# A two-layer encoder step: two more feed-forward tile buffers, the last gate's place, the tail weights' split and the norms' engines

## The chip, the cores and the metric

The kernel runs on one core of a Trainium2 chip, as one launch. The metric is the device time of that launch in microseconds (us). Engines: TensorE (PE; PEld is its weight load), VectorE (DVE), ScalarE (ACT), GpSimd (POOL) and SyncE (SP), which issues most of the DMAs. Each engine works through its instructions in the order in which the program emits them.

## The reference

A prompt of 1024 frames and a sample of 32 frames (T = 1056 columns here) go through two layers of width 1024. The first layer's mixer is a matrix-memory recurrence, the second one's is a sliding-window attention. After each mixer, and after each feed-forward block, comes a post-normalisation. The part that the change touches is this:

```python
def layer_norm(x, g, b):
    mu = jnp.mean(xf, -1, keepdims=True)
    var = jnp.mean(jnp.square(xf - mu), -1, keepdims=True)
    return (xf - mu) * lax.rsqrt(var + LN_EPS) * g + b

def swiglu(x, w_gu, w_down):            # D_FF = 2816
    g, u = jnp.split(x @ w_gu, 2, axis=-1)
    return (jax.nn.silu(g) * u) @ w_down

for layer in range(DEPTH):              # DEPTH = 2
    mix = mixer(layer, x)               # mLSTM, then sliding-window attention
    x = layer_norm(DEEPNORM_ALPHA * x + mix, ln_g[layer, 0], ln_b[layer, 0])
    x = layer_norm(DEEPNORM_ALPHA * x + swiglu(x, w_gu[layer], w_down[layer]),
                   ln_g[layer, 1], ln_b[layer, 1])
```

## The kernel before, in words

Everything is kept transposed: features on the 128 partitions, frames along the free axis. `ACT` holds the residual stream, `SX` its split into a rounded high part and a low part (fp32r). A product of two f32 matrices is three fp32r matmuls: high times high, high times low, low times high (L361, L362, L363 in `gemm`).

**Weights.** `Weights` streams them: SP loads a raw tile `wr` (three buffers), ScalarE casts the high part `wh` (L201), and GpSimd or, for the keys in `on_vector`, VectorE subtracts to get the low part `wl` (L203). Five such pairs of slots exist, and some weights have a home elsewhere (`ex`). For pairs of units, VectorE also makes sums of weights (L174 to L180). A raw tile is loaded anew when its last subtraction has read it. `done` releases a factor and emits the next ones at once.

**Order.** The program is emitted by Python generators. `Weave.tick` is called from `gemm` with an estimate of the time of three matmuls and steps each launched task when its pause has run out; `drain` runs a task at once to its end or to a condition. So what a task yields decides where its instructions stand in each engine's queue, not when they run.

**Feed-forward.** The 1056 columns are four quarters of 264 (`N4`). Tiles 0 and 1 of the 22 are made plainly, tiles 2 to 21 by `up_tile` with seven products in place of eight (a Strassen-like scheme) into PSUM banks A and B. Each tile takes buffers of `Z` from the list `free`: `s0` for the gate, `su0`, `su1` for the up parts, `s1` for the second gate. `alloc` takes one, and when none is free it drains the oldest staging task until one is. `stage(p)` combines tiles 2p and 2p+1, splits each combination (L1269 cast, L1270 subtraction) into buffers 7 to 10 in turn, and sends it to DRAM (`hs`, L1271); a buffer of the two tiles comes free with t1, x11, t4 and x22. The last Silu of a tile and its product (L1370, L1371) are in the task `rest`, which is launched after the last product. `behind` is set for the last tile alone: it starts loading the staged tiles back (L1413) while that tile is made.

The down product runs over four blocks with seven products each (`down`, L1465 and L1467 add into `ACT`), and a fifth, the tail, is done plainly for one quarter after the other (`run` in `ffn`, L1525), with the eight tail units `dn[TAIL]` from `dnt`.

**Norms.** `norm_tail` makes the quarters and launches `ln_task` for each. Its `li` is 1 and 3 behind the feed-forward blocks of the two layers. Per quarter: partial sums (L601, L603), a matmul with `onesm` for the mean (L422), centring (L427), squares (L429), their sums (L431, L434), a matmul for the variance (L438), the reciprocal root (L444 to L449), scaling (L453, L459 to L463), and the split for the next product (L469, L475). `LN_PACE` gives the pauses, `LN_LAG` adds to the one ahead of the variance matmul. In the last norm of the kernel quarter 2 is made with the pauses of `RUSH` (`rush`), and quarter 3 by `LastNorm`. After layer 0 the key, value and query products of the attention run between the steps of the last norms (`keys_values`, `q_group`); the attention's first steps come behind them (L1693 scores, L1699 their sums with the bias).

Of the kernel before, what the change touches and what calls it, by code (L numbers as in the profile page):

```python
# [9 lines left out]
F32 = mybir.dt.float32  # L10
# [6 lines left out]
P = 128  # L17
# [37 lines left out]
    ((4.2, 0.9, 1.1, 4.4, 1.0, 1.4, 0.8), (4.2, 0.7, 0.9, 4.2, 0.8, 1.4, 0.8)),  # L55
)

LN_LAG = {(2, 0): 7.0}

RUSH = (3.2, 0.8, 0.6, 2.8, 0.8, 1.0, 0.6)  # L60

# [3 lines left out]
N4 = T // 4  # L65
# [176 lines left out]
def kernel(ctx: ExitStack, tc: tile.TileContext, A, O):  # L242
# [14 lines left out]
    def new(p, tag, shape, dt=F32, bufs=1):  # L257
        uid[0] += 1
        return p.tile(list(shape), dt, name=f"{tag}_{uid[0]}", tag=tag, bufs=bufs)
# [29 lines left out]
    def add_ffn(layer):  # L289
        up, dn = {}, []  # L290
        for c, i in VISITS:
            held = up.get((i, 1 - c)) if i == FIRST - 1 else None
            up[i, c] = held or [add("gu", 2 * (layer * FT + i) + k) for k in range(2)]
        for i in range(FIRST, FT):
            up[i] = add_pair("gu", 2 * (layer * FT + i))
        for b in range(TAIL):
            dn.append([add_pair("dn", 4 * (layer * TAIL + b) + 2 * j) for j in range(2)])
        dn.append([add("dnt", KT * layer + m) for m in range(KT)])
        on_vector.update((u, 1) for u in dn[TAIL])
        on_vector.update((u, f) for i in range(FIRST) for c in range(2) for u in up[i, c] for f in range(2))  # L300
        U_UP.append(up)
        U_DN.append(dn)
# [100 lines left out]
    def ln_task(z_, lps, grp, li, last, final):  # L403
        cols, (c, zs) = grp
        w = cols.stop - cols.start

        rush = final and grp is QUARTERS[2]
        y = RUSH if rush else LN_PACE[li & 1][last]
        acc = z_[:, 0:2, c, zs]
        sq = [acc] + [z_[:, 2 + 2 * i : 4 + 2 * i, c, zs] for i in range(3)]  # L410
        rs, r2 = z_[:, 8, c, zs], z_[:, 9, c, zs]
        n = KT // 2

        def z2(kk):
            return ACT[:, 2 * kk : 2 * kk + 2, cols]

        def s2(i, kk):
            return SX[:, i, 2 * kk : 2 * kk + 2, cols]

        yield y[0]  # L420
        pm = new(lps, "ln", [P, 512], bufs=3 if li & 1 else 2)[:, :w]
        nc.tensor.matmul(pm, onesm[:], acc[:, 0, :], start=True, stop=True)  # L422
        yield y[1]
        for s in range(n + 2):
            if s < n:

                nc.vector.tensor_sub(z2(s), pm.unsqueeze(1).broadcast_to([P, 2, w]), z2(s))  # L427
            if 1 <= s <= n:
                nc.scalar.activation(sq[s - 1], z2(s - 1), AF.Square)  # L429
            if s >= 3:  # L430
                (nc.gpsimd if rush or li & 1 and not (last or s & 1) else nc.vector).tensor_add(acc, acc, sq[s - 2])  # L431
            yield y[2]
        if not rush:
            nc.vector.tensor_add(acc[:, 0], acc[:, 0], acc[:, 1])  # L434
        yield y[3] + LN_LAG.get((li, cols.start // N4), 0.0)
        pv = new(lps, "ln", [P, 512], bufs=3 if li & 1 else 2)[:, :w]
        for i in range(1 + rush):
            nc.tensor.matmul(pv, onesm[:], acc[:, i, :], start=(i == 0), stop=(i == rush))  # L438
        squared.add((li, cols.start // N4))
        yield y[4]  # L440

        if not li & 1:
            nc.scalar.preload_act_table_set("natural_log_exp_and_others")
        nc.scalar.activation(rs, pv, AF.Ln, bias=eps_ln[:])  # L444
        nc.scalar.activation(rs, rs, AF.Exp, scale=-0.5)
        nc.scalar.activation(r2, rs, AF.Square, scale=0.5 ** 0.5)
        yield y[5]
        nc.vector.scalar_tensor_tensor(r2, pv, eps_ln[:], r2, op0=ALU.add, op1=ALU.mult)
        nc.vector.scalar_tensor_tensor(rs, r2, 1.5, rs, op0=ALU.subtract, op1=ALU.mult)  # L449
        for s in range(n + 3):  # L450
            if s < n:
                eng = nc.gpsimd if rush and s & 1 else nc.vector
                eng.tensor_mul(z2(s), z2(s), rs.unsqueeze(1).broadcast_to([P, 2, w]))  # L453
            kk = s - 1
            if 0 <= kk < n:
                for k in (2 * kk, 2 * kk + 1):
                    z, gk, bk = ACT[:, k, cols], lng[:, li, k : k + 1], lnb[:, li, k : k + 1]
                    if rush and k & 1:
                        nc.gpsimd.tensor_scalar(z, z, gk, bk, op0=ALU.mult, op1=ALU.add)  # L459
                    elif li & 1 and last and k & 1:  # L460
                        nc.vector.tensor_scalar(z, z, gk, bk, op0=ALU.mult, op1=ALU.add)
                    else:
                        nc.scalar.activation(z, z, AF.Identity, scale=gk, bias=bk)  # L463
            kk = s - 2
            if 0 <= kk < n:
                if final:
                    nc.sync.dma_start(O["y"][:, 2 * kk : 2 * kk + 2, cols], z2(kk))
                else:
                    nc.scalar.copy(s2(0, kk), z2(kk))  # L469
                    if li == 1:  # L470
                        nc.scalar.dma_start(scr[:, 2 * kk : 2 * kk + 2, cols], z2(kk))
            kk = s - 3
            if kk >= 0 and not final:
                eng = nc.gpsimd if kk & li & 1 else nc.vector
                eng.tensor_sub(s2(1, kk), z2(kk), s2(0, kk).bitcast(F32))  # L475
            yield y[6]

    class LastNorm:
# [574 lines left out]
    class Mixer(ExitStack):  # L1053
# [3 lines left out]
        def __init__(self, closing, us):  # L1057
            super().__init__()
            closing()
            psx[0].close()  # L1060
            dense_psum(4)
            self.ex, self.zx = ExitStack(), ExitStack()
            self.E = new(self.ex.enter_context(pool("ex")), "ex", [P, 2, 3 * KT // 2, HALF], F32R)
            self.z = new(self.zx.enter_context(pool("z", side="right")), "z", [P, 11, 2, N4])
            self.lnps = self.enter_context(pool("lnps", PSUM, side="right"))
            self.made, self.plain, self.left = [], [False, False], 0
            for i, u in zip((0, 4, 1, 5, 2, 3), us):
                for f in range(2):
                    W.home[u, f] = [self.E[:, h, 2 * i + f, : D // 2] for h in range(2)]
# [149 lines left out]
    def ffn(layer, li, tasks, lx, final):  # L1219
# [19 lines left out]
        def tiles(t):  # L1239
            return [(t[:, 0, k, :], t[:, 1, k, :]) for k in range(t.shape[2])]  # L1240

        free = list(range(6))
        kept = {}
        staging = []
        turn = [0]
# [8 lines left out]
        def buf(i):  # L1256
            return Z[:, i, :, :]
# [65 lines left out]
        def up_tile(i, behind=None):  # L1323
            u = up[i]

            def mul(ps, f, o, **kw):
                w = tiles_of(W.factor(u, f))
                if i == FIRST and o[0] == "t":
                    summed(o)
                for c in range(2):  # L1330
                    gemm(ps[:, c, :], w, tiles(X[o](c)), **kw)
                W.done(u, f)
                if behind:
                    behind(o)

            a = bank("A")
            mul(a, "a1", "x11")
            finish_tile()
            s0 = alloc()
            gate0 = buf(s0)  # L1340
            nc.scalar.copy(gate0, a)
            if i > FIRST and not i % 2:
                staging.append(wv.launch(stage(i // 2 - 1)))
            b = bank("B")
            mul(b, "a2", "x21")
            nc.vector.tensor_add(gate0, gate0, b)
            nc.scalar.activation(gate0, gate0, AF.Silu)
            mul(a, "s2", "t2", again=True)
            su0 = alloc()
            up0 = buf(su0)  # L1350
            nc.scalar.copy(up0, a)
            b = bank("B")
            mul(b, "b2", "t4")
            nc.vector.tensor_add(up0, up0, b)
            mul(a, "s1", "t1", again=True)
            su1 = alloc()
            up1 = buf(su1)
            nc.scalar.copy(up1, a)  # L1358
            b = bank("B")
            mul(b, "s3", "t3")  # L1360
            nc.vector.tensor_add(up0, up0, b)
            nc.vector.tensor_add(up1, up1, b)
            nc.vector.tensor_mul(gate0, gate0, up0)
            free.append(su0)
            mul(a, "s4", "x22", again=True)
            s1 = alloc()
            kept[i] = s0, s1

            def rest():
                nc.scalar.activation(buf(s1), a, AF.Silu)  # L1370
                nc.vector.tensor_mul(buf(s1), buf(s1), up1)  # L1371
                free.append(su1)
                yield 0.5

            tail.append(wv.launch(rest()))
# [595 lines left out]
```

## Time and profile before

| | us |
|---|---|
| runs, median of 3 | 2244.7 |
| lowest and highest | 2244.04, 2245.94 |
| profiled execution, its own time | 2244.99 |
| its span, first to last instruction | 2242.9 |
| TensorE busy in it | 2187.7 |
| VectorE busy | 1472.7 |
| ScalarE busy | 999.6 |
| GpSimd busy | 1018.3 |

The profile is of one execution. A row of the waits gives who waited for whom, the time in all, how often, and the longest. A row of a timeline gives the start in us from the span's beginning, the duration, engine, line, operation and tiles, and in brackets how long the engine was idle before and what ended that. A row of the windows gives the stretch, its length, and for PE, PEld, DVE, ACT and POOL the busy time and the instructions in it, then the granted clock of TensorE, the busy share of the DMA engines, and GB/s. A row of the groups gives the count, the busy time, the mean in ns, and idle time before them. L203 is line 203 of the kernel before.

### The profile page before, as it was taken

The page shows a single profiled execution, that of the slowest core. Times are in us where ns is not written, and L with a number is a line of the kernel's source. Part 1 is how long each engine was busy: PE and PEld are TensorE (multiplying, and loading weights), DVE is VectorE, ACT ScalarE, POOL GpSimd, SP SyncE. Part 2 cuts the span into 40 slices and gives each one's busy share as a digit, 9 for nine tenths or more (in the row PEclk, how much of TensorE's full clock was granted, in tenths as well). Part 3 has the DMA queues.
Part 4 walks back from the last instruction along what each step waited for, and adds up shares of the span by engine and source line. Part 5 has one row for each costly group of instructions (what it writes and reads, how often), then busy time and mean ns, then how long its engine had stood idle before and what let it go on. Part 6 is the DMA issues. An engine that isn't in the chain of part 4 may idle for free.

```text
span 2242.9 us, 44249 instructions
## 1 busy us (share of the span) xinstructions
PE 2187.7 (98%) x17086; PEld 2151.6 (96%) x17086; DVE 1472.7 (66%) x2864; ACT 999.6 (45%) x2253; POOL 1018.3 (45%) x961
## 2 busy tenths in 40 slices
PE   9999999999999999999998999899999999999997
PEld 9899999999999999999998999899999999999997
DVE  4465576777566665566667678888666666456657
ACT  4443355465344444322246678656444444332124
POOL 2544331003665666545326676400566666554422
PEclk9999999999999999999999999999999999999999
DMA  4222112211443443697425433421344434397712
GB/s 149 75 54 69 53 40 86 96 39 58 165 138 140 154 152 137 230 332 232 153 79 169 115 99 95 138 78 39 106 154 160 139 134 154 135 347 242 257 50 78
DMA packets 174499, 298.10 MB, mean 133 GB/s; under 512 B 18065, under 2 KB 130761, under 8 KB 174289
## 3 DMA queue, kind: packets, MB, share of 16 engines
q1 hardware_dynamic: 169936, 290.94, 39.1%
q10 hardware_dynamic: 4352, 4.33, 0.6%
q8 instruction: 135, 2.21, 0.4%
q14 instruction: 76, 0.61, 0.1%
HBM read 201.80 MB, written 82.94 MB: 127 GB/s over the span
## 4 chain that ended last, share of the span: by engine, by line
PE 80%; DVE 8%; ACT 4%; DMA 3%; issue 3%; POOL 1%; SPq 0%; ACTq 0%; DVEq 0%; POOLq 0%
PE A L361 9%; PE A L363 9%; PE A L362 9%; PE d L361 8%; PE d L363 8%; PE d L362 8%; PE B L361 7%; PE B L362 7%; PE B L363 7%; PE T L1737 1%; DMA wr<-in_dn 1%; ACT act L463 1%; PE T L906 1%; PE O L1752 1%; DVE wl L203 1%
## 5 line engine op out<-in xcount | busy, mean ns | idle before, releaser
L203 POOL TENSOR_TENSOR wl_s<-wr,wh_s 128x512 fp32r<-128x512 f32 x224 | 316.6, 1434 | 243.0 <-ACT wh_s L201 182.6
L361 PE MATMUL d<-sx,wh 128*128 128x264 f32 (+2 forms) x1068 | 341.1, 319 | 0.7 <-DVE act L1525 0.7
L363 PE MATMUL d<-sx,wl 128*128 128x264 f32 (+2 forms) x1068 | 326.2, 305 | 1.4 <-POOL wl L203 1.4
L362 PE MATMUL d<-sx,wh 128*128 128x264 f32 (+2 forms) x1068 | 325.3, 305 | 0.1
L203 POOL TENSOR_TENSOR wl_a<-wr,wh_a 128x512 fp32r<-128x512 f32 x112 | 169.0, 1515 | 331.2 <-ACT wh_a L201 329.5
L201 ACT CAST wh_s<-wr 128x512 fp32r<-128x512 f32 x224 | 135.4, 617 | 310.9 <-DVE wr L178 279.4
L361 PE MATMUL A<-sx,wh_s 128*128 128x264 f32 x896 | 255.4, 285 | 3.5 <-ACT z L1358 3.5
L362 PE MATMUL A<-sx,wh_s 128*128 128x264 f32 x896 | 254.9, 284 | 0.0
L363 PE MATMUL A<-sx,wl_s 128*128 128x264 f32 x896 | 254.8, 284 | 0.0
L361 PEld LDWEIGHTS d<-sx,wh 128*128 128x128 f32 x1068 | 202.6, 190 | 4.3 <-ACT z L444 1.1
L363 PEld LDWEIGHTS d<-sx,wl 128*128 128x128 f32 x1068 | 201.6, 189 | 2.5 <-POOL wl L203 2.2
L362 PEld LDWEIGHTS d<-sx,wh 128*128 128x128 f32 x1068 | 202.3, 189 | 1.1 <-DVE sx L392 0.4
L363 PE MATMUL d<-sx,ex 128*128 128x264 f32 x624 | 177.7, 285 | 3.5 <-DVE ex L203 3.5
L361 PE MATMUL d<-sx,ex 128*128 128x264 f32 x624 | 180.6, 289 | 0.4 <-ACT sx L391 0.2
L203 POOL TENSOR_TENSOR wl<-wr,wh 128x512 fp32r<-128x512 f32 (+2 forms) x75 | 100.1, 1344 | 177.5 <-ACT wh L201 154.5
L362 PE MATMUL d<-sx,ex 128*128 128x264 f32 x624 | 177.3, 284 | 0.3 <-DVE sx L392 0.2
L361 PEld LDWEIGHTS A<-sx,wh_s 128*128 128x128 f32 x896 | 169.3, 189 | 4.0 <-ACT z L1358 4.0
L363 PEld LDWEIGHTS A<-sx,wl_s 128*128 128x128 f32 x896 | 169.6, 189 | 0.0
L362 PEld LDWEIGHTS A<-sx,wh_s 128*128 128x128 f32 x896 | 169.2, 189 | 0.0
L1270 POOL TENSOR_TENSOR z<-z 128x528 fp32r<-128x528 f32 x76 | 105.3, 1385 | 109.2 <-issue 58.0
L1717 POOL TENSOR_SCALAR s<-s,st 128x256 f32<-128x256 f32 (+1 forms) x144 | 126.6, 891 | 61.3 <-DVE st L1715 47.6
L1269 ACT CAST z<-z 128x528 fp32r<-128x528 f32 x136 | 85.9, 631 | 95.5 <-DVE z L1282 44.9
(338 smaller groups left out, 7299.3 us busy)
## 6 DMA issues: line engine op xcount, KB each, us to landing
wr<-in_gu SPq DMA_DIRECT2D x92, 512.0 KB, 4.9
hs_x<-z SPq DMA_DIRECT2D x72, 528.0 KB, 2.8
hs_t<-z SPq DMA_DIRECT2D x64, 528.0 KB, 2.9
sx<-hs_x SPq DMA_DIRECT2D x112, 264.0 KB, 5.9
sx<-hs_t SPq DMA_DIRECT2D x64, 264.0 KB, 6.4
ex<-hs_t SPq DMA_DIRECT2D x64, 264.0 KB, 6.4
wr<-in_dn SPq DMA_DIRECT2D x32, 512.0 KB, 3.9
ex<-hs_x SPq DMA_DIRECT2D x32, 264.0 KB, 5.9
```

Of the source, the lines that this page charges most:

```text
L201: self.nc.scalar.copy(hi, r)
L203: eng.tensor_sub(lo, r, hi.bitcast(F32))
L361: nc.tensor.matmul(out, ah, bh, start=start and k == 0, stop=False, **kw)
L362: nc.tensor.matmul(out, ah, bl, start=False, stop=False, **kw)
L363: nc.tensor.matmul(out, al, bh, start=False, stop=stop and k == last, **kw)
L463: nc.scalar.activation(z, z, AF.Identity, scale=gk, bias=bk)
L906: nc.tensor.matmul(pc[:, : 2 * (DV + 1)], keys, vt[j][:L, c], start=True, stop=True)
L1269: nc.scalar.copy(hi.bitcast(F32R), buf(s))
L1270: eng.tensor_sub(lo.bitcast(F32R), buf(s), hi)
L1717: nc.gpsimd.tensor_scalar_mul(p[:R, h, lo:256], p[:R, h, lo:256], st[:R, 2, h : h + 1])
L1737: nc.tensor.transpose(pt[:nk, i, h, :R], p[:R, h, c : c + nk], ident[:R, :R])
L1752: nc.tensor.matmul(po[:, :, :R], v, s["hi"][:nk, i, :, :R], start=(i == 0), stop=False)
```

## The change

The buffer `Z` has 13 tiles in place of 11, and the list `free` starts with eight buffers in place of six. In the last tile the second gate's Silu is emitted behind its last product and ahead of `W.done`, which emits the next weights' casts; in the other tiles it stays in `rest`. The second half of the tail weights is no longer in `on_vector`, so GpSimd makes both low parts. In `ln_task` the additions L431 stay on GpSimd in the rushed quarter alone; of the scalings, L453 and the odd steps of the rushed quarter leave GpSimd (for VectorE and ScalarE), and all of L475 is on VectorE. `LN_LAG` adds 1.0 and 1.2 us of ticks ahead of the variance matmul in quarters 2 and 3 behind the first feed-forward block.

```diff
-LN_LAG = {(2, 0): 7.0}
+LN_LAG = {(1, 2): 1.0, (1, 3): 1.2, (2, 0): 7.0}
...
         dn.append([add("dnt", KT * layer + m) for m in range(KT)])
-        on_vector.update((u, 1) for u in dn[TAIL])
...
             if s >= 3:
-                (nc.gpsimd if rush or li & 1 and not (last or s & 1) else nc.vector).tensor_add(acc, acc, sq[s - 2])
+                (nc.gpsimd if rush else nc.vector).tensor_add(acc, acc, sq[s - 2])
...
             if s < n:
-                eng = nc.gpsimd if rush and s & 1 else nc.vector
-                eng.tensor_mul(z2(s), z2(s), rs.unsqueeze(1).broadcast_to([P, 2, w]))
+                nc.vector.tensor_mul(z2(s), z2(s), rs.unsqueeze(1).broadcast_to([P, 2, w]))
...
-                    if rush and k & 1:
-                        nc.gpsimd.tensor_scalar(z, z, gk, bk, op0=ALU.mult, op1=ALU.add)
-                    elif li & 1 and last and k & 1:
+                    if li & 1 and last and k & 1:
                         nc.vector.tensor_scalar(z, z, gk, bk, op0=ALU.mult, op1=ALU.add)
...
             if kk >= 0 and not final:
-                eng = nc.gpsimd if kk & li & 1 else nc.vector
-                eng.tensor_sub(s2(1, kk), z2(kk), s2(0, kk).bitcast(F32))
+                nc.vector.tensor_sub(s2(1, kk), z2(kk), s2(0, kk).bitcast(F32))
...
-            self.z = new(self.zx.enter_context(pool("z", side="right")), "z", [P, 11, 2, N4])
+            self.z = new(self.zx.enter_context(pool("z", side="right")), "z", [P, 13, 2, N4])
...
-        free = list(range(6))
+        free = [*range(6), 11, 12]
...
-            def mul(ps, f, o, **kw):
+            def mul(ps, f, o, then=None, **kw):
...
                 for c in range(2):
                     gemm(ps[:, c, :], w, tiles(X[o](c)), **kw)
+                if then:
+                    then()
                 W.done(u, f)
...
-            mul(a, "s4", "x22", again=True)
             s1 = alloc()
             kept[i] = s0, s1
 
+            def gate1():
+                nc.scalar.activation(buf(s1), a, AF.Silu)
+
+            mul(a, "s4", "x22", behind and gate1, again=True)
+
             def rest():
-                nc.scalar.activation(buf(s1), a, AF.Silu)
+                if not behind:
+                    gate1()
                 nc.vector.tensor_mul(buf(s1), buf(s1), up1)
                 free.append(su1)
                 yield 0.5
```

## The prediction

> **What bounds the kernel now.** I read the busy shares of the page first, then the waits of TensorE, then the windows around each long wait, then the timelines there.
>
> ```profile
> PE 2187.7 (98%) x17086; PEld 2151.6 (96%) x17086; DVE 1472.7 (66%) x2864; ACT 999.6 (45%) x2253; POOL 1018.3 (45%) x961
> ```
>
> The waits of TensorE (in all, times, longest, us), those that the change can touch:
>
> ```profile
> PE psS L1693 <- DVE st L1699: 3.7, 2, 3.1
> PE A L361 <- ACT z L1358: 3.5, 2, 1.9
> PE d L363 <- DVE ex L203: 3.5, 6, 1.1
> PE A L361 <- ACT z L1370: 3.0, 2, 1.8
> ...
> PE ln L438 <- DVE z L434: 2.1, 2, 1.1
> PE ln L555 <- DVE z L544: 2.1, 1, 2.1
> ```
>
> TensorE (PE) is the bound: busy 98%. Its matmuls do not change, so only its waits are to be had; 2242.9 − 2187.7 = 55 us is idle, start and end included. Six kinds of wait are shown, and each edit aims at one or two. Next to them stands what a quiet stretch looks like:
>
> ```profile
> 560.00:580.00 20.00, 18.07 (x136) 17.86 (x135) 10.00 (x12) 7.54 (x15) 11.62 (x10) 0.91 0.54 188
> 600.00:620.00 20.00, 20.00 (x167) 20.00 (x166) 12.23 (x14) 8.36 (x16) 12.59 (x9) 1.00 0.44 162
> 940.00:960.00 20.00, 18.78 (x155) 18.57 (x154) 12.80 (x17) 6.07 (x11) 11.68 (x8) 1.00 1.08 374
> 1180.00:1200.00 20.00, 18.30 (x105) 17.66 (x105) 15.87 (x27) 10.81 (x21) 9.02 (x9) 0.91 0.42 131
> 1600.00:1620.00 20.00, 18.38 (x152) 18.17 (x151) 9.94 (x13) 8.39 (x16) 11.97 (x9) 1.00 0.54 189
> 1980.00:2000.00 20.00, 18.17 (x150) 17.96 (x149) 12.86 (x18) 6.33 (x12) 11.68 (x8) 1.00 1.06 354
> ```
>
> A full 20 us holds 167 matmuls of this shape, 0.12 us each. Missing matmuls times 0.12 is therefore the true loss of a stretch, with pipeline drain and lowered clock in it.
>
> **Two more buffers (free list of 8).** Tiles 0 and 1 keep four of the six buffers; every later tile takes four (`s0`, `su0`, `su1`, `s1`) and returns two. From the code this is arithmetic on ticks: a product is 8 ticks of 0.339 = 2.7, a tile seven products = 19.0; the staging of a pair returns a buffer at ticks 2, 12.4, 28 and 33.2 (t1, x11, t4, x22). An odd tile asks for `su1` after five of its products, 19.0 + 13.6 = 32.6 after the even tile began, and what it gets is the buffer of t4. Pairs from 1 on start staging one product into an even tile: 2.7 + 28 = 30.7, in time. Pair 0 starts after four products of tile 2: 10.8 + 28 = 38.8, too late. So once per layer, in tile 3, `alloc` finds the list empty and drains two puts back to back. With eight buffers one is left even there, and no drain occurs.
>
> ```profile
> 570.10 0.63 ACT L1269 CAST z<-z 128x528 fp32r<-128x528 f32 x1 [4.58 <-DMA hs_t<-z]
> 571.56 0.60 ACT L1358 COPY z<-A 128x528 f32<-128x528 f32 x1 [0.83 <-DVE z L1270]
> ```
>
> The drained put sits ahead of the copy that frees bank A: ScalarE waits 4.58 us for the earlier put's DMA, then for VectorE, and TensorE waits 1.9 us for the copy. Gone with the drain are (167 − 136) × 0.12 = 3.7 us in layer 0 (half of it the clock: 0.91 over 20 us is 0.09 × 20 = 1.8) and (167 − 152) × 0.12 = 1.8 in layer 1: **−5.5**. Next late: the put of x22 now falls 5.4 ticks behind that of t4, on the same staging buffer, and one round trip there was 4.58 us of waiting plus work; a late landing would hold ScalarE some 2 us, but the copy behind it has one whole product (24 × 0.12 = 2.9 us) before its bank is used. So nothing is charged; if that cover failed, 2 us a layer.
>
> The Trainium skill (TensorE: Matmul & The Clock Gate, section on HAM oscillation) would have the clock fall only for idle gaps above some 3.4 us. This trace differs: 0.91 follows a 1.9 us wait. By the page the sum below would be 1.8 us smaller; the measured row decides.
>
> **Last gate ahead of the release.** The last tile's Silu (L1370) frees bank A for the first down product, but is emitted behind a weight cast.
>
> ```profile
> 945.91 0.62 ACT L201 CAST wh_s<-wr 128x512 fp32r<-128x512 f32 x1 [3.45 <-PE A L363]
> 946.44 0.60 ACT L1370 ACTIVATE z<-A 128x528 f32<-128x528 f32 x1
> ```
>
> The same stretch on VectorE and GpSimd, then the chain some 10 us later:
>
> ```profile
> 945.13 0.69 DVE L178 TENSOR_TENSOR wr<-wr,wr 128x512 f32<-128x512 f32 x1
> 947.08 1.38 DVE L1371 TENSOR_TENSOR z<-z 128x528 f32<-128x528 f32 x1 [1.25 <-ACT z L1370]
> 947.85 1.80 POOL L1270 TENSOR_TENSOR z<-z 128x528 fp32r<-128x528 f32 x1
> ```
>
> ```profile
> 957.86 6.82 DMA wr<-in_dn
> 964.68 0.28 issue
> 964.96 0.69 DVE wr L174
> 965.65 0.63 DVE act L1465
> ```
>
> The cast waits for L178, which ends at 945.82, while ScalarE idles 3.45 us in which the Silu fits; behind it now stands that cast, which L178 holds until then anyway. Losses removed: (167 − 155) × 0.12 = 1.4 and (167 − 150) × 0.12 = 2.0. But I read on for what is late next. At 957.86 SP, in its order behind the last pair's staging puts, issues the next down weights (6.82 us); then comes L174, and behind it on VectorE the L1465 that frees bank A again. Coming 1.4 or 2.0 us earlier, it waits for the same load. That chain starts from L1270; L1371 runs beside it until 948.46, 0.6 of its 1.80 us, and will now run before it. So only about 0.5 us a layer stays: **−1.0**, bounds 0 and −3.4; I take the low part as the DMA share is 1.08 there.
>
> **Tail weights on GpSimd alone.** Of the 8 tail units a layer, the second half's subtraction leaves VectorE.
>
> ```profile
> L203 POOL TENSOR_TENSOR ex<-wr,ex 128x384 fp32r<-128x384 f32 x6 | 6.1, 1018 | 13.9 <-ACT ex L201 13.9
> ```
>
> ```profile
> 1116.09 0.43 DVE L1525 TENSOR_TENSOR act<-act,d 128x264 f32<-128x264 f32 x1 [1.76 <-PE d L363]
> 1116.44 1.35 DVE L203 TENSOR_TENSOR ex<-wr,ex 128x384 fp32r<-128x384 f32 x1
> ```
>
> VectorE is not slow, it is in the wrong order: L203 for a unit to come stands behind L1525, which waits for TensorE's end of the unit before (1.76). Raw loads wait for these subtractions too. GpSimd has 13.9 us idle before its six, so six more of 1.02 (6.1) fit; a pair takes 2.04 against a unit's 18 × 0.12 = 2.2 us. With raw buffers freed by GpSimd, it runs units ahead; behind its subtractions stand only those of the next weights. The waits were 3.5 us on matmuls in two layers; resuming costs about 0.1 each time, six times: **−4.2**. Bounds −3.5 and, GpSimd late, the rival below.
>
> **Norms on VectorE, two held steps.**
>
> ```profile
> L475 DVE TENSOR_TENSOR sx<-act,sx 128x528 fp32r<-128x528 f32 x40 | 30.0, 760 | 14.0 <-ACT sx L469 14.0
> ...
> L431 POOL TENSOR_TENSOR z<-z 128x528 f32<-128x528 f32 x8 | 10.6, 1326 | 63.9 <-ACT z L429 63.0 <-DVE z L431 0.7
> ```
>
> And on VectorE, at quarters 2 and 3 of the first layer:
>
> ```profile
> 1184.27 0.71 DVE L431 TENSOR_TENSOR z<-z 128x528 f32<-128x528 f32 x1 [1.19 <-POOL z L431]
> ...
> 1217.64 1.80 DVE L475 TENSOR_TENSOR sx<-act,sx 128x528 fp32r<-128x528 f32 x1
> ```
>
> Five of the eight L431 and all eight L475 of GpSimd (steps 1 and 3 of four quarters) move, 0.75 each on VectorE. In layer 0 that is 3 + 8 = 11 × 0.75 = 8.3 us more work. Against it, VectorE waited 1.19 for one L431, and lost 1.80 − 0.76 = 1.0 when its L475 ran beside GpSimd's. At quarter 2 it gains 1.19 and what is shortened, less two operations of 0.7: about 0.4. The held matmul (1.0 tick, two steps of the next product; L444 to L449 of its norm stand behind it) no longer stands in the way, but the bank of that product waits for VectorE as well. At quarter 3 the hold of 1.2 removes the 1.1 us wait for L434, yet TensorE then comes earlier to the attention's scores, where it waits 3.1 for L1699, the end of the same norm chain; I credit 0.6 for a chain not interrupted. Together **−1.0**. Bounds: +3 (both holds delay the chain, 2.2, and 0.8 of backlog) and −2.7 (the second half-speed stretch, 0.91 at 1180, is not entered: 1.7 more). I take the middle, since every wait here ends on VectorE.
>
> The rushed norm of the last layer moves two L453 to VectorE and four scale steps to ScalarE, just ahead of TensorE's last long wait.
>
> ```profile
> L453 DVE TENSOR_TENSOR act<-act,z 128x528 f32<-128x528 f32 x2 | 1.4, 704 | 0.0
> ```
>
> ```profile
> 2223.68 1.31 DVE L540 TENSOR_TENSOR z<-z,act 128x528 f32<-128x528 f32 x1
> ...
> 2227.32 1.41 DVE L544 TENSOR_TENSOR z<-z 128x264 f32<-128x264 f32 x1
> 2228.65 0.42 DVE L558 TENSOR_TENSOR act<-act,d 128x264 f32<-128x264 f32 x1
> ```
>
> VectorE gets 1.4 us more (2 × 704 ns), and L540 (0.6) and L544 (1.0) shrink to free durations (0.7, and 0.42 as L558 has it), with 0.3 between: 1.9 back, **−0.5**. Bounds: 0, if ScalarE with its four steps comes late with the squares in between, and −0.8.
>
> **Sum.** −5.5 − 1.0 − 4.2 − 1.0 − 0.5 = −12.2. The profiled execution took 2244.99 (its span 2242.9), the median of the runs is 2244.7: 2244.99 − 12.2 = 2232.8, rounded to 2233.0.
>
> **The rivals.**
> 1. *More is kept.* The down weights also land earlier (2.4 us more of the gate's 3.4) and the half-speed stretch at 1187 goes (1.7): 2228.9. Against it: DMA share 1.08.
> 2. *GpSimd becomes the bound of the tail.* Its L1270 above took 1.80, 0.6 of it beside VectorE's work; 1.02 in that measure (× 1.5, half of it hidden: × 1.37) is 1.4, which makes a pair 2.8 against 2.2. Six units lose 3.6 a layer, less one unit's lead (2.2): 4.2 + 2 × 1.4 = 7.0 given back, 2240.0. It decides once a subtraction exceeds 1.1. The Trainium skill (SBUF — State Buffer, section Who interferes with whom) has this as a rule: two-operand VectorE work and GpSimd's reads exclude each other, and the one issued first wins. For it speaks L203's 1.35 us on VectorE; against, the six rows' mean of 1018.
> 3. *The buffers do not do what they say*, a drain still being forced somewhere: 5.5 back, 2238.5. Against it: the count has one drain, and the view has one wait per layer.
> 4. *Slower: VectorE's backlog in the first layer's norms reaches the attention.* All 11 moved operations (8.3) and both holds (2.2) land on the chain that ends in L1699, its longer waits lower the clock three more times (3 × 1.7), and the 1.0 is lost: 16.6 back, 2249.6. It decides once the backlog passes 12 us. For it: VectorE busy 15.87 of 20 us at 1180. Against: 4.13 us were idle there, and GpSimd's share blocked it anyway.
>
> **How the numbers follow.** Chances: forecast 0.62, rival 1 0.14, rival 2 0.09, rival 3 0.06, rival 4 0.05, other small losses between 2237 and 2243 0.04. The range 2226.5 to 2239.5 takes in the forecast with the bounds of its norms and gate terms, rivals 1 and 3. About 0.2% (4.5 us) is what a measurement of this kernel can tell from no change: faster needs less than 2240.5. That is forecast, rivals 1 and 3 and most of rival 2: 0.88. Same gets 0.08; slower, past 2249.5, 0.04.
>
> **What would show it.** Right: no wait of TensorE for L1358's counterpart, and granted clock 1.00 around 570; none on `ex` from L203; no wait for the last Silu, but a longer one, 1.5 to 2 us, for L1465 some 20 us later in both layers; the wait for L1699 grown towards 4 us while those for L434 are gone; L544 near 0.5. Wrong: waits of TensorE on GpSimd's `ex`, new clock losses between 1180 and 1440, or a wait in tile 3 or 4 of either layer.

## The result: 6 us faster, half of the forecast, and the profile after

| | before | after |
|---|---|---|
| median of 12 runs each, us | 2244.43 | 2238.71 |
| lowest to highest | 2240.66 to 2246.44 | 2236.94 to 2240.69 |
| ratio, 95% interval | | 0.9973 (0.9966 to 0.9981) |
| profiled execution, its span | 2244.99, 2242.9 | 2237.53, 2235.7 |

The ratio is 6.1 us (4.3 to 7.6) off 2244.7. Forecast were 12, to 2233.0, with a range of 2226.5 to 2239.5: the sign held and the time is inside the range, near its slow end. Later ratios are likewise turned into us by 2244.7, since the kernel before drifted from 2244 to 2247 between the groups of runs.

In the changed kernel the lines have moved: `gemm` is L360 to L362, the squares' sums L430 and L433, the split L470, the tail's eviction L1527, the copies L1338, L1348 and L1355, the down additions L1467 and L1469, the scores' sums L1701. TensorE's waits in the profile after (in all, times, longest, us):

```profile
PE psS L1695 <- DVE st L1701: 5.7, 1, 5.7
...
PE A L360 <- DVE act L1467: 3.3, 2, 1.7
...
PE d L360 <- DVE act L1527: 2.3, 1, 2.3
PE d L362 <- POOL wl L203: 2.1, 3, 0.8
...
PE ln L550 <- DVE z L539: 1.3, 1, 1.3
PE ln L437 <- DVE z L433: 1.3, 1, 1.3
...
PE A L360 <- ACT z L1348: 1.1, 2, 0.7
```

Gone are the waits on `ex`, for the last Silu and for L1358's counterpart (L1355). In their place stand a longer one for the down additions, a new one (L1348), the one for the tail's eviction (L1527), grown from 0.7 to 2.3, and one of 5.7 for the scores' sums. Two of the prediction's own signs of being wrong are there: L1348 is a wait in tile 4 of both layers, and the clock at 1200 to 1220 is 0.90 where it was 1.00 (at 1180 to 1200 it is 1.00 where it was 0.91). By windows (columns as before):

```profile
560.00:580.00 20.00, 20.00 (x167) 20.00 (x166) 9.68 (x12) 7.75 (x14) 11.18 (x9) 1.00 0.39 134
580.00:600.00 20.00, 19.28 (x159) 19.07 (x158) 11.79 (x15) 9.35 (x17) 12.72 (x11) 1.00 0.56 190
940.00:960.00 20.00, 20.00 (x167) 20.00 (x167) 13.82 (x21) 6.21 (x12) 12.41 (x9) 1.00 1.08 374
960.00:980.00 20.00, 18.38 (x152) 18.20 (x151) 13.21 (x21) 4.25 (x7) 9.36 (x7) 1.00 1.07 378
1200.00:1220.00 20.00, 12.81 (x71) 12.29 (x72) 17.64 (x26) 11.64 (x26) 13.28 (x11) 0.90 0.76 223
```

TensorE runs the same 17086 matmuls in both traces, almost in the same order, so one can ask where the same matmul starts in each. Its shift (after minus before), read on the level stretches ahead of each place and behind it, gives the account; a third number is what is left of a gain some 15 to 20 us later:

| stretch | shift from, to (us) | the change's term | forecast |
|---|---|---|---|
| ahead of the first feed-forward | 0, +0.97 | +1.0 | 0 |
| buffers, layer 0 (572; then 588) | +0.97, −2.77, −1.77 | −2.7 | −3.7 |
| gate, layer 0 (947; then 966) | −1.77, −3.25, −1.82 | −0.1 | −0.5 |
| tail weights, layer 0 | −1.80, −4.55 | −2.75 | −2.1 |
| norms and attention (1135 to 1235; by 1600) | −4.55, −2.38, −2.23 | +2.3 | −1.0 |
| buffers, layer 1 (1613; then 1628) | −2.23, −4.08, −3.33 | −1.1 | −1.8 |
| gate, layer 1 (1987; then 2006) | −3.33, −5.43, −3.84 | −0.5 | −0.5 |
| tail weights, layer 1 | −3.83, −6.33 | −2.5 | −2.1 |
| end | −6.33, −7.13 | −0.8 | −0.5 |

The first row is code that the change doesn't touch, so it is put down to chance between two executions. Without it this pair of traces gives −8.1; the timed runs say −6.1. Such chance is in the other rows too, above all between 1135 and 1600, where the clock falls two to four times in every trace.

### The profile page after: what moved, and what is told of

It is laid out like the page before. It is cut to its first block, busy times and chain, and to the rows that moved or that the text cites. A ratio compares the mean times of both kernels' runs of the same rounds, so it can differ in the third digit from the quotient of the medians.

```text
span 2235.7 us, 44254 instructions
## 1 busy us (share of the span) xinstructions
PE 2182.9 (98%) x17086; PEld 2149.4 (96%) x17086; DVE 1468.5 (66%) x2863; ACT 999.8 (45%) x2257; POOL 1008.0 (45%) x958
## 4 chain that ended last, share of the span: by engine, by line
PE 62%; DVE 4%; issue 2%; DMA 2%; ACT 2%; POOL 1%; SPq 0%; ACTq 0%; POOLq 0%; DVEq 0%
PE A L360 9%; PE A L362 9%; PE A L361 9%; PE B L360 6%; PE B L361 6%; PE B L362 6%; PE d L360 4%; PE d L362 4%; PE d L361 4%; PE T L1739 1%; DMA wr<-in_dn 1%; PE psS L1695 1%; PE O L1754 1%; PE psS L1696 1%; PE O L1755 1%
## 5 line engine op out<-in xcount | busy, mean ns | idle before, releaser
L360 PE MATMUL d<-sx,wh 128*128 128x264 f32 (+2 forms) x1068 | 341.4, 320 | 3.3 <-DVE act L1527 2.3
L362 PE MATMUL d<-sx,wl 128*128 128x264 f32 (+2 forms) x1068 | 326.0, 305 | 2.2 <-POOL wl L203 2.1
L360 PE MATMUL A<-sx,wh_s 128*128 128x264 f32 x896 | 254.9, 284 | 1.1 <-ACT z L1348 1.1
L362 PE MATMUL A<-sx,wl_s 128*128 128x264 f32 x896 | 254.0, 284 | 0.0
L360 PEld LDWEIGHTS d<-sx,wh 128*128 128x128 f32 x1068 | 202.3, 189 | 7.0 <-issue 2.8
L203 POOL TENSOR_TENSOR wl<-wr,wh 128x512 fp32r<-128x512 f32 (+2 forms) x79 | 104.7, 1333 | 224.3 <-ACT wh L201 210.2
L362 PEld LDWEIGHTS d<-sx,wl 128*128 128x128 f32 x1068 | 201.8, 189 | 3.3 <-POOL wl L203 3.1
L360 PE MATMUL d<-sx,ex 128*128 128x264 f32 x624 | 180.5, 289 | 0.2 <-DVE act L1197 0.2
L362 PE MATMUL d<-sx,ex 128*128 128x264 f32 x624 | 176.9, 284 | 0.0
L360 PEld LDWEIGHTS A<-sx,wh_s 128*128 128x128 f32 x896 | 168.4, 188 | 1.7 <-ACT z L1348 1.5
L362 PEld LDWEIGHTS A<-sx,wl_s 128*128 128x128 f32 x896 | 168.8, 188 | 0.0
```

The lines of the kernel that those rows point to most:

```text
L203: eng.tensor_sub(lo, r, hi.bitcast(F32))
L360: nc.tensor.matmul(out, ah, bh, start=start and k == 0, stop=False, **kw)
L362: nc.tensor.matmul(out, al, bh, start=False, stop=stop and k == last, **kw)
```

## The experiments

Each was timed in five rounds with runs of the kernel before beside it. An interval is some 2 us wide to each side, so the totals tell terms of 3 us apart and the traces have to tell the smaller ones.

**One part at a time, on the kernel before.**

```diff
-            self.z = new(... [P, 11, 2, N4])
+            self.z = new(... [P, 13, 2, N4])
-        free = list(range(6))
+        free = [*range(6), 11, 12]
```

> The kernel before with the two more tile buffers alone. As forecast: 5.5 us faster, 2238.9, with no forced drain and nothing late behind it. As the trace after reads (after the drain is gone TensorE waits 0.9 and 0.6 us, some 14 us later, for the copy L1348's counterpart): 4.1 us faster, 2240.3. If the drains were not forced by the list: no change.

Measured: 0.9985 (0.9975 to 0.9995), 3.4 us faster (1.1 to 5.6). In its trace the stretch 560 to 580 holds 167 matmuls, and two waits for the copy one place earlier in the tile stand behind it:

```profile
560.00:580.00 20.00, 20.00 (x167) 20.00 (x166) 9.66 (x12) 7.75 (x14) 10.99 (x9) 1.00 0.41 134
```

```profile
PE A L361 <- ACT z L1351: 1.5, 2, 1.1
```

That is the reading with the give-back rather than the forecast's, though the interval holds 5.5 too.

```diff
-            mul(a, "s4", "x22", again=True)
             s1 = alloc()
+            def gate1(): nc.scalar.activation(buf(s1), a, AF.Silu)
+            mul(a, "s4", "x22", behind and gate1, again=True)
```

> The kernel before with the last tile's gate ahead of the release alone. As forecast: 1.0 us faster, 2243.4, all but 0.5 us a layer being given back some 20 us later, where VectorE's addition (L1465) stands behind L174, which waits for the raw down weights. As the trace after reads: 0.2 us faster, 2244.2, a wait of 1.8 us a layer in place of one of 1.8. If the gain is kept whole: 3.4 faster, 2241.0.

Measured: 1.0 (0.9991 to 1.001): nothing (2.0 faster to 2.2 slower). Its trace has no wait for the last Silu, and this for the down addition:

```profile
PE A L361 <- DVE act L1472: 3.4, 2, 1.8
```

A gain of 1.4 and 2.0 came back as waits of 1.8 and 1.6. By the same matmul's place the first layer even loses 3.4 for the 1.5 gained, since the clock falls behind that wait (0.91 at 960 to 980). The forecast's 1.0 lies inside the interval; that the gain is kept whole does not.

```diff
-        on_vector.update((u, 1) for u in dn[TAIL])
```

> The kernel before with the tail weights' low parts on GpSimd alone. As forecast: 4.2 us faster, 2240.2, no wait on ex. As the trace after reads (the position of the same matmul moves by 2.75 and 2.4 us in the two tails): 5.1 faster, 2239.3. Rival: the chain of the first layer's last norm is a floor of its own, so that the first layer's share comes back as a longer wait for the scores' sums: 2.4 faster, 2242.0.

Measured: 0.9984 (0.9975 to 0.9992), 3.6 us faster (1.8 to 5.6). The trace has no wait of TensorE on `ex` any more. The two tails gain 2.7 and 2.5 us by the same matmul's place. But of the first layer's 2.7 only 0.4 is left behind the first scores and 1.3 at 1600, so the rival, whose 2.4 is inside the interval too, isn't refuted: part of that gain comes back in the norms. How much of it is the chain and how much the clock (0.83 at 1200 to 1220, 1.00 before) stays open. In the changed kernel GpSimd's subtractions take

```profile
L203 POOL TENSOR_TENSOR ex<-wr,ex 128x384 fp32r<-128x384 f32 x24 | 24.4, 1058 | 0.7 <-ACT ex L201 0.7
```

1058 ns in the mean, below the 1.1 from which it would have become the bound.

```diff
-LN_LAG = {(2, 0): 7.0}
+LN_LAG = {(1, 2): 1.0, (1, 3): 1.2, (2, 0): 7.0}
-  (nc.gpsimd if rush or li & 1 and not (last or s & 1) else nc.vector).tensor_add(acc, ...)
+  (nc.gpsimd if rush else nc.vector).tensor_add(acc, ...)
-  eng = nc.gpsimd if kk & li & 1 else nc.vector
-  eng.tensor_sub(s2(1, kk), ...)
+  nc.vector.tensor_sub(s2(1, kk), ...)
```

> The kernel before with the squares' sums (L431) and the splits (L475) on VectorE and the two holds (1.0 and 1.2) alone; the rushed quarter stays as it was. As forecast: 1.0 us faster, 2243.4. As the trace after reads (between the end of the tail and the first scores' sums the same matmul loses 2.2 us): 2.2 slower, 2246.6, with a wait of TensorE for L1699 above 4 us.

Measured: 1.0018 (1.0009 to 1.0027), 4.0 us **slower** (2.0 to 6.1). The forecast of this part had the wrong sign. Its trace names the place:

```profile
PE psS L1692 <- DVE st L1698: 5.8, 1, 5.8
PE d L361 <- DVE act L1524: 2.3, 1, 2.3
```

**Which of its edits, on the changed kernel and on the one before.**

```diff
-LN_LAG = {(1, 2): 1.0, (1, 3): 1.2, (2, 0): 7.0}
+LN_LAG = {(2, 0): 7.0}
```

> The changed kernel (2238.7) without the two holds of 1.0 and 1.2 in the first layer's norms. By the forecast, which credited the holds with about 0.6 at quarter 3 and nothing at quarter 2: 0.6 us slower, 2239.3. By the trace of the norms alone, where quarter 2's reciprocal root comes 1.0 us later although its sums end 1.6 us earlier: the holds lengthen the chain to the scores' sums, so 1.0 to 2.5 us faster, about 2237. If the whole price is VectorE's added work: no change.

Measured: 0.996 (0.9947 to 0.9972) of the kernel before, 9.0 us faster than it (6.3 to 11.9), where the changed kernel is 6.1 faster; the medians are 2235.46 and 2238.71. So the holds seem to cost about 3, not minus 0.6; the two intervals overlap a little, and by these totals alone a cost near nothing isn't excluded.

With the even steps' squares' sums back on GpSimd, and in another run the odd steps' splits:

> The changed kernel (2238.7) with the even steps' squares' sums back on GpSimd. By the forecast (VectorE waited 1.19 us for one of them at quarter 2): 0.4 us slower or the same, 2239.1. If the moved additions are the price, because the evictions of the tail stand behind them (TensorE waits 2.3 us for one of these in the changed kernel): 1.5 us faster, 2237.2.

> The changed kernel (2238.7) with the odd steps' splits (L475 before) back on GpSimd. By the forecast (each shortened one is worth about as much as the operation added): no change to 0.5 us slower, 2239.0. If the splits are the price, since the last quarter's three now stand in one run of 4.07 us ahead of the scores' sums in VectorE's queue: 1.5 to 2.7 us faster, about 2236.7.

Measured: 0.9976 (0.9966 to 0.9985) and 0.9975 (0.9966 to 0.9985), 5.4 and 5.6 us faster than before, against 6.1. So neither move alone is likely to be the price: the 1.5 us faster that either would then have brought lies at the edge of both intervals. Both runs sit on the forecast's side, and neither 0.5 us nor zero can be told from the other here.

```diff
+LN_LAG = {(1, 2): 1.0, (1, 3): 1.2, (2, 0): 7.0}      (the kernel before, else unchanged)
```

> The kernel before with the two holds alone, all engines as they were. If the holds by themselves lengthen the chain, as taking them out of the changed kernel (3.2 us faster) says: 3 us slower, about 2247.5. If they cost only beside VectorE's added work: no change. As the forecast had it: 0.6 us faster.

Measured: 1.0004 (0.9994 to 1.0013), 0.9 us slower (1.3 faster to 2.9 slower): between the first two readings, and 3 us is just outside. By totals alone this would be unclear. The chain itself is clearer. From the end of the sums of quarter 2's squares (L434, L433 after) to the first scores' sum (L1699, L1701 after) the traces have, in us, 34.8 before, 37.3 with the holds alone, 38.9 with the whole norm part, 38.2 in the changed kernel and 36.0 in it without the holds. In these five the holds add 2.5 and 2.2, the moves 1.6 and 1.2, whichever comes first. All fourteen traces together bear out the holds, but not the moves: the chain takes 37.3 to 39.0 in the seven kernels with a hold and 34.2 to 37.3 in the seven without (the 37.3 is the tail weights alone, which has neither holds nor moves); without the holds it is 35.3 to 36.6 with the moves and 34.2 to 37.3 without them. TensorE's own place agrees: from 1135 to 1600 the seven with a hold lose 2.1 to 5.3 us against the kernel before, the six others between 0.6 gained and 1.4 lost and, once, 3.9 lost (the last run below). Why the holds do is seen where it begins. ScalarE's first step of the reciprocal root in the kernel before:

```profile
1186.31 0.48 ACT L444 ACTIVATE z<-ln,eps_ln 128x264 f32<-128x264 f32 x1 [3.99 <-PE ln L438]
```

The changed kernel, TensorE, then VectorE, then that step on ScalarE:

```profile
1179.81 0.28 PE L362 MATMUL d<-sx,ex 128*128 128x264 f32 x1
1182.38 0.42 PE L360 MATMUL d<-sx,wh 128*128 128x384 f32 x1 [2.29 <-DVE act L1527]
...
1183.51 0.60 PE L437 MATMUL ln<-z,onesm 128*128 128x264 f32 x2
```

```profile
1180.34 0.47 DVE L433 TENSOR_TENSOR z<-z 128x264 f32<-128x264 f32 x1
1180.73 0.42 DVE L1527 TENSOR_TENSOR act<-act,d 128x264 f32<-128x264 f32 x1
1181.18 0.71 DVE L596 TENSOR_TENSOR z<-z,act 128x528 f32<-128x528 f32 x1
1181.81 0.76 DVE L1527 TENSOR_TENSOR act<-act,d 128x264 f32<-128x264 f32 x2
```

```profile
1184.15 0.48 ACT L443 ACTIVATE z<-ln,eps_ln 128x264 f32<-128x264 f32 x1 [5.55 <-PE ln L437]
```

The changed kernel without the holds, TensorE, then that step on ScalarE:

```profile
1181.32 0.68 PE L437 MATMUL ln<-z,onesm 128*128 128x264 f32 x2 [0.87 <-DVE z L433]
1182.74 0.41 PE L360 MATMUL d<-sx,wh 128*128 128x384 f32 x1 [0.74 <-DVE act L1527]
```

```profile
1182.04 0.48 ACT L443 ACTIVATE z<-ln,eps_ln 128x264 f32<-128x264 f32 x1 [3.07 <-PE ln L437]
```

The sums are ready at 1180.81 in the changed kernel. Because of the hold, TensorE has two steps of the key product ahead of the variance matmul, and that product's bank is held until the tail's last evictions (L1527), which VectorE reaches at 1181.8. So the matmul, ready at 1180.8, comes at 1183.5. TensorE gains nothing by it: one wait of 2.29 in place of 0.87 + 0.74. The root starts 3.3 us behind the sums instead of 0.9 (1186.31 behind sums that end at 1185.45, before; 1182.04 behind 1181.17, without the holds).

Later in the changed kernel VectorE and GpSimd also meet. Quarter 3's last three splits, ahead of the scores' sums in VectorE's queue, with the holds and without them, and GpSimd at that time in the changed kernel:

```profile
1214.37 4.07 DVE L470 TENSOR_TENSOR sx<-act,sx 128x528 fp32r<-128x528 f32 x3
```

```profile
1214.55 1.94 DVE L470 TENSOR_TENSOR sx<-act,sx 128x528 fp32r<-128x528 f32 x3
```

```profile
1214.82 3.05 POOL L203 TENSOR_TENSOR wl<-wr,wh 128x512 fp32r<-128x512 f32 x2 [1.48 <-ACT wh L201]
```

That the price hangs on this meeting is not shown: with quarter 2's hold alone (next) each of these splits takes 0.70 us, and the chain is as long.

With quarter 2's hold kept and quarter 3's dropped:

> The changed kernel (2238.7) with the hold of quarter 2 kept and that of quarter 3 dropped. If quarter 2's hold is the price (its reciprocal root comes late and the centring of quarter 3 stands behind it): no change, 2238.7. If quarter 3's is: as without both, 2235.5. If each pays its own length: 2237.2.

Measured: 0.9965 (0.9953 to 0.9977), 7.9 us faster (5.2 to 10.5): midway, and not told apart from the kernel with both or with neither. In its trace the chain is 38.9 us against 38.2 with both, VectorE's first step of quarter 2's root (L447) starts 5.8 us behind the sums (4.8 with both), and TensorE's wait for the scores' sums is shorter as it waits for quarter 3's L433 instead:

```profile
PE ln L437 <- DVE z L433: 2.8, 1, 2.8
PE psS L1695 <- DVE st L1701: 2.8, 2, 1.8
```

So its trace puts the price of the chain on quarter 2's hold; by time it stays open how it is shared.

**What the gate's gain waits for.**

```diff
-        def feed(pause):
+        def feed(pause, first=0.0):
+            if first:
+                yield first
...
-                feeding.append(wv.launch(feed(FEED)))
+                feeding.append(wv.launch(feed(FEED, 8.0)))        (in behind alone)
```

> The changed kernel (2238.7) with the loads of the second down block begun 8 us later, so that the raw down weights have SP's queue and the DMA engines more to themselves. If the given-back gain of the gate is the wait for those weights, as the forecast has it, the waits of 1.7 us a layer for the down products' addition vanish: 2.5 to 3.3 us faster, about 2235.8. If the weights' landing is set by what was already queued, or the second block's own loads then come late: no change, or 1 to 3 us slower.

Measured: 0.9954 (0.9941 to 0.9966), 10.3 us faster than before (7.6 to 13.2), 4 more than the changed kernel; the waits for the down addition are gone in both layers, and 960 to 980 is full where the changed kernel had 152:

```profile
960.00:980.00 20.00, 20.00 (x167) 20.00 (x167) 13.51 (x20) 4.77 (x8) 9.91 (x8) 1.00 1.05 359
```

ScalarE's cast that waits for the raw down weights, in the changed kernel and in this one:

```profile
963.17 0.62 ACT L201 CAST wh_b<-wr 128x512 fp32r<-128x512 f32 x1 [4.56 <-DMA wr<-in_dn]
```

```profile
960.78 0.62 ACT L201 CAST wh_b<-wr 128x512 fp32r<-128x512 f32 x1 [5.42 <-DMA wr<-in_dn]
```

The load is issued 0.6 us earlier (955.10 for 955.70), this cast starts 2.4 us earlier, and L174 follows at 961.27 in place of 963.15, while TensorE is at the same place to 0.1 us. The staging's last put comes earlier as well, but in the changed kernel VectorE had dealt with what stood behind it and waited another 0.64 us at L174.

**Both together, and a faster first pair.**

> The changed kernel without the holds and with the second block's loads 8 us later. If the two are independent: 2238.7 - 3.2 - 4.4 = 2231.1, that is 14 us below the kernel before. If part of the one comes back in the other's place: 2233 to 2235.

Measured: 0.9939 (0.9928 to 0.9951), 13.7 us faster (11.0 to 16.2).

```diff
-            pause = 5.2
+            pause = 4.6 if p == 0 else 5.2
```

> The same with pauses of 4.6 in place of 5.2 in the staging of the first pair, so that its last put falls ahead of the first put of the next pair. If the waits of TensorE for the copy L1348 (1.7 us in both layers) come from the two pairs' puts meeting: 1.2 to 1.7 us faster, about 2229.7. If the shorter pauses crowd another product: no change.

Measured: 0.9931 (0.9919 to 0.9943), 15.5 us faster (12.8 to 18.2), the best of all; from the step before it is not told apart by time. By the traces it does what it should in layer 0: without it, then with it,

```profile
580.00:600.00 20.00, 18.32 (x150) 18.11 (x150) 12.19 (x15) 8.87 (x17) 13.14 (x10) 1.00 0.54 190
```

```profile
580.00:600.00 20.00, 20.00 (x167) 20.00 (x167) 14.86 (x15) 9.22 (x17) 14.75 (x10) 1.00 0.47 154
```

and no wait for that copy is left in either layer.

## Why the prediction was right in sign and half in size

**Buffers: right mechanism, 5.5 forecast, 3.4 measured, 3.8 by the traces.** Two things were mis-sized. First, the 3.7 of layer 0 counted 1.8 us of lowered clock as a consequence of the wait. The kernels with the gate, the tail weights, the norms and the holds alone still have the drain; in their traces, in this order, the stretch reads

```profile
560.00:580.00 20.00, 18.66 (x153) 18.45 (x153) 10.42 (x12) 8.16 (x15) 12.20 (x10) 1.00 0.52 188
```

```profile
560.00:580.00 20.00, 18.22 (x150) 18.01 (x149) 9.72 (x12) 8.39 (x15) 11.76 (x10) 1.00 0.54 188
```

```profile
560.00:580.00 20.00, 18.06 (x149) 17.85 (x148) 9.57 (x12) 8.38 (x15) 11.63 (x10) 1.00 0.53 188
```

```profile
560.00:580.00 20.00, 17.87 (x136) 17.66 (x135) 9.59 (x12) 7.82 (x15) 11.22 (x10) 0.91 0.53 188
```

In three of them the clock stays at 1.00 and the loss is 14 to 18 matmuls, 1.7 to 2.2 us; of the five traces with the drain, two have the lowered clock (the last section shows what decides it). Its cost belongs into the term with that share, 0.7 and not 1.8. Second, "nothing is charged" for what is late next was wrong: of the 2 us a layer named for the case that the cover fails, 1.0 and 0.75 came. What fills ScalarE is not a late landing (0.17 us of idle time) but two puts within one product, the next pair's first and the first pair's last, ahead of the copy:

```profile
582.97 0.63 ACT L1264 CAST z<-z 128x528 fp32r<-128x528 f32 x1 [3.64 <-issue]
...
584.85 0.63 ACT L1264 CAST z<-z 128x528 fp32r<-128x528 f32 x1 [0.17 <-DMA hs_t<-z]
...
585.91 0.59 ACT L1348 COPY z<-A 128x528 f32<-128x528 f32 x1
```

**Gate: right.** The gain came back at the addition behind L174, 17 to 18 us later in both layers, and the delayed loads showed that the raw weights' landing was what it waited for. Whether the 0.5 a layer is kept (the table has 0.1 and 0.5) is below what can be resolved.

**Tail weights: right.** 4.2 forecast (its terms, 3.5 and six times 0.1, make 4.1), 3.6 measured, 5.25 at the two tails in the trace of the whole change. What the forecast left out is that the first layer's share runs into the norm chain behind it, where some of it may come back, as in the trace of this part alone.

**Norms: the step that failed.** Minus 1.0 was forecast, with bounds of +3 and −2.7; measured was +4.0 (2.0 to 6.1). The sentence that "the bank of that product waits for VectorE as well" named the mechanism, and then no price was put on it: behind a hold the variance matmul waits for that bank too. Why the part costs 4.0 where the holds' chain explains 2.2 to 2.5 stays open; the interval is wide enough for both. The bound on the holds took their own length, 2.2 in all, and landed at the measured 2.2 to 2.5 of the chain; the value chosen was the opposite sign. Of the credit of 0.4 at quarter 2 for additions moved off GpSimd, 0.1 came: the sums end 1.0 us behind the start of the tail's last matmul after, 1.1 before. The bound of +3 was the better number.

**End: right**, 0.8 by the trace against 0.5; L539 takes 0.43 us where L544 took 1.41. It was not run by itself.

**The sum.** The parts measured alone give −3.4 + 0 − 3.6 + 4.0 = −3.0, with the end some −3.8, against −6.1 for all of them; each has 2 us of interval to either side, so nothing speaks for or against an interaction. Of the 6 us missing from the forecast, some 3 to 5 are the norms, and about 2 the buffers. None of the four rivals happened. Rival 1 would have needed the down weights early, as the delayed loads then made them; rival 4 had the right place, the chain to the scores' sums, and its 2.2 for the holds came, but not its 8.3 for the moved operations. That the total fell inside the range is partly luck: the norms' bound of +3 alone reaches 2237.0, and the 2 us that the buffers kept back, for which nothing was charged, came on top.

## What to carry to other kernels

Holding an instruction back so that an engine does other work first pays only if that other work can start: look up what frees its first operand, here the bank behind the very queue that the hold was meant to cover. A gain ahead of a load is kept only if the load comes earlier too, so move the load with it; delaying traffic that isn't urgent by 8 us of ticks was worth about as much as the change's largest part. And a loss that contains a lowered clock is to be taken from several traces before it is credited, because the same gap lowers it in one execution and not in the next.

## What the runs showed of the hardware

The clock is not set by a wait's length alone. The wait for L1358 lowered it to 0.91 where it was 1.9 us (before) and 2.1 us (holds alone), and not where it was 1.8 and 1.9 us (tail weights alone, norms alone). In the first mixer, which no version touches, TensorE waits 1.8 us for VectorE at the same place, before and then after,

```profile
PE T L906 <- DVE act L955: 1.8, 1, 1.8
```

```profile
PE T L901 <- DVE act L950: 1.8, 1, 1.8
```

and yet the windows around it read, before and then after:

```profile
310.00:330.00 20.00, 17.91 (x110) 15.65 (x109) 14.24 (x47) 9.84 (x35) 2.84 (x2) 1.00 0.12 34
```

```profile
310.00:330.00 20.00, 18.21 (x104) 15.90 (x103) 14.39 (x46) 9.67 (x33) 2.84 (x2) 0.91 0.11 34
```

Where it falls, matmuls go to half speed (0.32 us apart in place of 0.18 for the 384 columns) for some 3.4 us and cost about 1.7. The page TensorE: Matmul & The Clock Gate of the Trainium skill (section on HAM oscillation) has the clock fall only for idle gaps above some 3.4 us; in these traces single gaps of 1.9 and 2.1 us sometimes did it. So did a pair of gaps of about 0.9 and 0.7 us close together at 1180 to 1190, in the kernel before and in the changed one without the holds (0.91 in both); the same pair in the kernels with the buffers, the gate and the tail weights alone left 1.00.

What decides it can be worked out from the fourteen traces. In each of them all the times at which the clock falls lie whole multiples of 3.413 us apart: before, at 572.99, 1187.39, 1221.52 and 1439.97, which is 180, 10 and 64 of them. So each trace can be cut into cells of that length, and the cells begin elsewhere in each execution. Before, the wait for L1358 (570.28 to 572.21) lies inside one cell, and the next cell runs at half speed:

```profile
569.58:572.99 3.41, 1.48 (x12) 1.27 (x12) 2.23 (x4) 2.06 (x4) 0.23 (x1) 1.00 0.31 124
572.99:576.40 3.41, 3.41 (x18) 3.41 (x18) 3.34 (x3) 0.22 (x1) 2.79 (x2) 0.50 0.18 72
```

With the norms alone a wait as long (570.85 to 572.79) is split between two cells, and none does:

```profile
568.32:571.73 3.41, 2.53 (x21) 2.32 (x20) 1.01 (x2) 0.63 (x1) 0.00 (x0) 1.00 0.44 168
571.73:575.14 3.41, 2.35 (x19) 2.35 (x20) 3.41 (x6) 1.65 (x3) 1.80 (x2) 1.00 0.39 159
575.14:578.55 3.41, 3.41 (x30) 3.41 (x30) 2.46 (x3) 0.76 (x2) 1.28 (x2) 1.00 0.40 159
```

Counted over all cells at full clock ahead of 2150 us: each of the 32 in which TensorE was idle for 1.9 us or more was followed by half speed, 15 of the 55 with 1.55 to 1.88 us were, and none of the 8647 with less. By this count a gap of 1.9 us costs clock where it falls into one cell, which is an estimated (3.41 − 1.9) / 3.41 = 0.44 of all places, near the two in five seen above; and two short gaps count together if they share a cell (1.70 us in the one ahead of 1187.39, before).
